# A decoder layer on one core: idle products and idle accumulating loads in the first feed-forward

## The chip, the cores and the metric

The kernel runs on one core of a Trainium2 chip. A core has engines that each work through an instruction queue of their own, in order: TensorE (PE in the profile, its weight loads PEld), VectorE (DVE), ScalarE (ACT), GpSimd (POOL) and SyncE (SP, which here only starts transfers). They wait for each other through semaphores. Transfers between the large memory and the on-chip memory are started by SP, ACT or POOL and carried out by 16 DMA engines that all queues share. The metric is the device time of one execution in microseconds (us); a lower time is better.

## The reference, cut to what matters

The layer works on 272 tokens (16 learned meta tokens and 256 of the sequence) of width 2048, in float32:

```python
s = concat([meta, x])                                   # 272 x 2048
h = rms_norm(s, norm_ffn1)
s = s + 0.5 * swiglu_ffn(h, ffn1_w_gu, ffn1_w_down)     # first feed-forward, width 5632
h = rms_norm(s, norm_mix)
q, k, v, b_gate, c_gate, u = split(h @ w_in)
y_att, y_conv = diff_attention(q, k, v, ...), short_conv(b_gate, c_gate, u, conv_w)
s = s + (sum of gated (y_att, y_conv) @ w_branch) @ w_out
h = rms_norm(s, norm_ffn2)
s = s + 0.5 * swiglu_ffn(h, ffn2_w_gu, ffn2_w_down)     # second feed-forward
return rms_norm(s, norm_final)[16:]

def swiglu_ffn(h, w_gu, w_down):
    gate, up = split(h @ w_gu)
    return (silu(gate) * up) @ w_down
```

## The kernel before

Every large product is computed from rounded halves. The type F32R is a rounded float32 that TensorE takes in one pass. Each weight block `st` is rounded on ACT to `wh` (L258) and the rest `wl = st - wh` is made on DVE (L259); activations are kept in the same way as a high and a low part. One weight chunk of 128 rows by 128 columns then needs three products: high times high (L267), high times low (L268) and low times high (L269).

`linear` does one group of 512 output columns: it goes through the 16 chunks of 128 rows of the contraction in 8 blocks of two chunks, and keeps four accumulators (one PSUM bank each) of 272 tokens. A block of two chunks is 2 x 4 x 3 = 24 products of 272 columns, and a whole `linear` is 192. The buffers `wh` and `wl` are three deep, so ACT can round block n only when TensorE is through with block n - 3. The raw block `st` is four deep, with four chunks in each.

In the first feed-forward, `gate_up` calls `linear` twice for each group g: once for the gate (accumulators `pg`) and once for the up part (`pu`). What follows a `linear` (its evict function) is put in `pending` and is emitted while the next `linear` runs, after its chunk 1 (`EVICT_AT`). Small work of another kind is put in the list `side`; each `linear` takes one entry of it after its chunks 5, 9 and 13. Below, pg0, pu0, pg1, pu1, pg2 name the first five `linear` calls in order, and pu1 block 3 the fourth block of two chunks of pu1.

In pg0 the kernel also prepares its input block by block (`before1`); with the last block it puts `make_vec` and `lam_step` in `side`. They are taken in pu0 after chunks 5 and 9. Nothing else is in `side` then until the end of the first feed-forward.

The scratch tiles of tag `wide` are three deep; `sg`, which holds the gate of one group until its up part is done, is one of them. The emitted instructions are ordered for each engine by a scheduler that works at build time. The input `s` lies in four tiles `sF`.

Of the kernel before, what the change touches and what calls it, by code (L numbers as in the profile page):

```python
# [9 lines left out]
F32 = mybir.dt.float32  # L10
F32R = mybir.dt.float32r
AF = mybir.ActivationFunctionType
ALU = mybir.AluOpType
AX = mybir.AxisListType

P = 128
# [5 lines left out]
DC = D // P  # L22
GC = 4
GW = GC * P
# [18 lines left out]
def decoder_layer(ctx: ExitStack, tc: tile.TileContext, t, out):  # L43
    nc = tc.nc

    const = ctx.enter_context(tc.tile_pool(name="const", bufs=1))
    wpool = ctx.enter_context(tc.tile_pool(name="w", bufs=W_BUFS))
    apool = ctx.enter_context(tc.tile_pool(name="a", bufs=N_ACT))
    tmp = ctx.enter_context(tc.tile_pool(name="tmp", bufs=2))
    psum = ctx.enter_context(tc.tile_pool(name="ps", bufs=8, space=bass.MemoryType.PSUM))  # L50

    def bank(name):
        return psum.tile([P, 512], F32, tag="acc", name=name)

    def wide(shape, name):
        return tmp.tile(shape, F32, tag="wide", bufs=3, name=name)
# [16 lines left out]
    def load_x(k):  # L73

        q, cs = k // 2, slice(k % 2 * GW, (k % 2 + 1) * GW)
        for i in range(2):
            nc.sync.dma_start(out=xin[q][i][:, cs], in_=x[i * P : (i + 1) * P, k * GW : (k + 1) * GW])
# [9 lines left out]
    def load_gain(g0, src):  # L87
# [5 lines left out]
        out=vrows[G_CONV:G_SUB, :], in_=t["conv_w"][0].rearrange("k (c p) -> (k c) p", p=P)  # L93
# [3 lines left out]
    for i, n in enumerate(("lambda_q1", "lambda_k1", "lambda_q2", "lambda_k2")):  # L97
# [7 lines left out]
        out=mask[:, T - P :],  # L105
        in_=mask[:, T - P :],
# [13 lines left out]
    def col(i):  # L120
        return vec[:, i : i + 1]
# [9 lines left out]
    def make_lam():  # L131
        lprod = tmp.tile([P, 2, HD], F32, tag="lprod", bufs=1, name="lprod")
        nc.vector.tensor_mul(lprod, lamv[:, 0:4:2, :], lamv[:, 1:4:2, :])
        ldot = const.tile([P, 2], F32, name="ldot")
        nc.vector.tensor_reduce(out=ldot, in_=lprod, axis=AX.X, op=ALU.add)
        lexp = const.tile([P, 2], F32, name="lexp")
        nc.scalar.activation(lexp, ldot, AF.Exp)
        nc.vector.tensor_sub(lam, lexp[:, 0:1], lexp[:, 1:2])
        nc.vector.tensor_scalar_add(lam, lam, LAM_INIT)
        nc.vector.tensor_scalar_mul(subg, col(G_SUB), 1.0 - LAM_INIT)  # L140


    sF = [apool.tile([P, GC, T], F32, tag="act", name=f"s{g}") for g in range(DC // GC)]
# [26 lines left out]
    def gain_split(h, c, gain):  # L170

        w = h.width
        hi, lo = h.part(c, 0, 0, w), h.part(c, 1, 0, w)
        a = nc.scalar.mul(hi, s(c, T - w), gain)
        b = nc.vector.scalar_tensor_tensor(
            out=lo, in0=s(c, T - w), scalar=gain, in1=hi.bitcast(F32), op0=ALU.mult, op1=ALU.subtract
        )
        return a.ins, b.ins
# [50 lines left out]
    side = []  # L229
# [179 lines left out]
    h1 = Act("h1", DC, T)  # L409
    norm1 = Norm(0, "1")  # L410

    def prep(c):
        pt = bank("pt")
        q, cs = c // NH, slice(c % NH * P, (c % NH + 1) * P)
        nc.tensor.transpose(pt[:, :NMETA], xm[q][:, cs], ident[:NMETA, :NMETA])
        for i in range(2):
            nc.tensor.transpose(pt[:, NMETA + i * P : NMETA + (i + 1) * P], xin[q][i][:, cs], ident)
        v = nc.vector.tensor_copy(s(c, 0), pt[:, :T])
        a, b = gain_split(h1, c, gain1[:, c : c + 1])
        return a, v.ins  # L420

    def before1(blk):


        c = blk[0]
        if c // 2 + 1 < 4:
            load_x(c // 2 + 1)
        r = []
        for k in blk:
            a, v = prep(k)  # L430
            r = [a, v]
        if c:
            for k in blk:
                norm1.add(k - 2)
        if c == DC - 2:
            for k in blk:
                norm1.add(k)
            pending.append(norm1.end)
            side.append(make_vec)

            def lam_step():
                with tc.issue_after(norm1.last.ins):
                    make_lam()

            side.append(lam_step)
        return r


# [3 lines left out]
    def after1(c):  # L452
        gain_split(h2, c, col(G_MIX + c))
        norm2.add(c)
        if c == DC - 1:
            side.append(norm2.end)

    for half in halves:
        m = gate_up(h1, half, t["ffn1_w_gu"][0], norm1, 0, before1 if half is halves[0] else None)
        for c in range(0, DC, GC):  # L460

            def down(pd, c=c, final=half is halves[-1]):
                for j in range(GC):
                    nc.vector.scalar_tensor_tensor(
                        out=s(c + j, 0), in0=pd[j][:, :T], scalar=0.5, in1=s(c + j, 0), op0=ALU.mult, op1=ALU.add
                    )
                    if final:
                        after1(c + j)

            linear(m, list(range(len(half) * GC)), t["ffn1_w_down"][0], half[0] * GC, c * P, 0, T, "pd", down)  # L470
# [265 lines left out]
    for half in halves:  # L736
        m = gate_up_tok(h3, half, w_gu, norm3)
        final = half is halves[-1]
        if final:
            for q in range(2):  # L740
                nc.gpsimd.dma_start(
                    out=gfin[q],
                    in_=t["norm_final"][q * W2 : (q + 1) * W2].rearrange("(o d) -> o d", o=1).to_broadcast([P, W2]),
# [46 lines left out]
```

## Time and profile before

| What | Value |
|---|---|
| time, median of 2 runs | 2233.66 us (2233.38 to 2233.95) |
| span of the profiled execution, from first to last instruction | 2231.4 us |
| what the runs' median has beside that span | 2.3 us |
| PE busy | 2215.7 us (99%), 14014 matmul records |
| DVE busy | 1268.5 us (57%) |
| ACT busy | 979.2 us (44%) |
| POOL busy | 6.4 us, 17 instructions |
| mean granted TensorE clock | 0.999 |
| moved by DMA | 401.98 MB, 180 GB/s over the span |

The profiled execution has no time of its own listed beside its span, so its own time is taken as the span and the 2.3 us around it. The trace stamps every instruction with a start and a duration. Products on TensorE are pipelined: a product is listed with some 0.29 us, though the next one begins 0.125 us later, so the cost of a product is read from start to start.

### The profile page before, as it was taken

The numbers are of one execution on the slowest core, as the hardware profiler recorded it, in microseconds if no ns is written. First come the engines' busy times: TensorE is split into PE (matmuls) and PEld (weight loads), VectorE is DVE, ScalarE is ACT, GpSimd is POOL, SyncE is SP. The second block draws the span as 40 slices with busy tenths as digits, with TensorE's granted clock in tenths as the row PEclk, the third lists the DMA queues.
The fourth block names the chain that finished last, engine by engine and source line by source line (L and its number), as shares of the span: only waits on it lengthen the run. The fifth ranks groups of instructions, "written<-read, shape, count | busy, mean of one in ns | idle before, by whom it ended". The sixth has DMA issues, their size and how long they took to land.

```text
span 2231.4 us, 33637 instructions
## 1 busy us (share of the span) xinstructions
PE 2215.7 (99%) x14014; PEld 2017.6 (90%) x14014; DVE 1268.5 (57%) x1681; ACT 979.2 (44%) x1238; POOL 6.4 (0%) x17
## 2 busy tenths in 40 slices
PE   9999999999999999999999999999999999999998
PEld 8999999999999999898988888888888888888886
DVE  7555554455555565667766665665555545455554
ACT  6444343334343443544455454544444433444443
POOL 0000000000000000000000000000000000000000
PEclk9999999999999999999999999999999999999999
DMA  7555555545555555444455555555555556555553
GB/s 232 173 181 176 171 172 181 176 170 175 181 174 170 175 178 177 151 152 151 153 195 187 188 184 192 186 189 189 188 189 189 189 189 214 199 185 192 189 182 120
DMA packets 191257, 401.98 MB, mean 180 GB/s; under 512 B 7908, under 2 KB 7968, under 8 KB 191104
## 3 DMA queue, kind: packets, MB, share of 16 engines
q1 hardware_dynamic: 190464, 398.49, 53.3%
q8 instruction: 109, 1.79, 0.3%
q0 software_dynamic: 544, 1.21, 0.2%
q14 instruction: 44, 0.36, 0.0%
q10 hardware_dynamic: 96, 0.14, 0.0%
HBM read 397.71 MB, written 2.10 MB: 179 GB/s over the span
## 4 chain that ended last, share of the span: by engine, by line
PE 99%; ACT 0%; DVE 0%; DMA 0%; issue 0%; ACTq 0%
PE pg L301 7%; PE pg L303 7%; PE pg L302 7%; PE g L265 5%; PE pg L269 4%; PE pg L267 4%; PE pd L269 4%; PE pu L269 4%; PE pu L267 4%; PE pg L268 4%; PE pd L267 4%; PE pu L268 4%; PE pd L268 4%; PE pd L303 4%; PE pd L301 4%; PE pd L302 4%
## 5 line engine op out<-in xcount | busy, mean ns | idle before, releaser
L259 DVE TENSOR_TENSOR wl<-st,wh 128x1024 fp32r<-128x1024 f32 x488 | 596.2, 1225 | 538.1 <-ACT wh L258 537.4
L258 ACT CAST wh<-st 128x1024 fp32r<-128x1024 f32 x488 | 514.0, 1054 | 731.2 <-PE pd L268 146.5
L319 DVE TENSOR_TENSOR wl<-st,wh 128x1024 fp32r<-128x1024 f32 x264 | 323.1, 1225 | 343.1 <-ACT wh L318 343.0
L318 ACT CAST wh<-st 128x1024 fp32r<-128x1024 f32 x264 | 278.6, 1055 | 411.6 <-PE pg L302 268.7
L301 PE MATMUL pg<-wh,h 128*128 128x512 f32 x704 | 276.0, 392 | 0.0
L303 PE MATMUL pg<-wl,h 128*128 128x512 f32 x704 | 274.2, 390 | 0.0
L302 PE MATMUL pg<-wh,h 128*128 128x512 f32 x704 | 273.9, 389 | 0.0
L267 PE MATMUL pg<-h,wh 128*128 128x272 f32 x704 | 203.5, 290 | 2.0 <-ACT wh L258 2.0
L267 PE MATMUL pu<-h,wh 128*128 128x272 f32 x704 | 203.2, 289 | 0.0
L269 PE MATMUL pd<-m,wl 128*128 128x272 f32 x704 | 203.0, 288 | 0.0
L269 PE MATMUL pu<-h,wl 128*128 128x272 f32 x704 | 203.0, 288 | 0.0
L267 PE MATMUL pd<-m,wh 128*128 128x272 f32 x704 | 203.0, 288 | 0.0
L268 PE MATMUL pu<-h,wh 128*128 128x272 f32 x704 | 202.4, 288 | 0.0
L268 PE MATMUL pg<-h,wh 128*128 128x272 f32 x704 | 202.4, 288 | 0.0
L268 PE MATMUL pd<-m,wh 128*128 128x272 f32 x704 | 202.4, 287 | 0.0
L269 PE MATMUL pg<-h,wl 128*128 128x272 f32 x704 | 201.2, 290 | 0.0
L265 PE MATMUL g<-h,wh 128*128 128x512 f32 x512 | 180.1, 395 | 0.0
L303 PEld LDWEIGHTS pg<-wl,h 128*128 128x128 f32 x704 | 132.1, 188 | 27.8
L302 PEld LDWEIGHTS pg<-wh,h 128*128 128x128 f32 x704 | 132.2, 188 | 26.8
L301 PEld LDWEIGHTS pg<-wh,h 128*128 128x128 f32 x704 | 132.2, 188 | 26.7
L269 PE MATMUL g<-h,wl 128*128 128x256 f32 x512 | 143.4, 280 | 0.0
L301 PE MATMUL pd<-wh,m 128*128 128x512 f32 x352 | 137.3, 390 | 0.0
(229 smaller groups left out, 4109.1 us busy)
## 6 DMA issues: line engine op xcount, KB each, us to landing
st<-in_ffn_w_gu_dram SPq DMA_DIRECT2D x184, 512.0 KB, 4.2
st<-in_ffn_w_down_dram SPq DMA_DIRECT2D x88, 1024.0 KB, 5.1
st<-in_ffn_w_gu_dram SPq DMA_DIRECT2D x84, 1024.0 KB, 4.9
st<-in_w_in_dram SPq DMA_DIRECT2D x48, 1024.0 KB, 5.1
st<-in_w_gate_dram SPq DMA_DIRECT2D x32, 1024.0 KB, 5.1
st<-in_w_branch_dram SPq DMA_DIRECT2D x16, 1024.0 KB, 5.0
st<-in_w_out_dram SPq DMA_DIRECT2D x16, 1024.0 KB, 5.0
xin<-in_x_dram SPq DMA_DIRECT2D x8, 256.0 KB, 7.3
```

The lines of the kernel that those rows point to most:

```text
L258: nc.scalar.copy(out=wh[:, :m, :], in_=sw)
L259: nc.vector.tensor_sub(wl[:, :m, :], sw, wh[:, :m, :].bitcast(F32))
L265: nc.tensor.matmul(acc[j][:, : 2 * n], wh[:, i, f], act.both(c, t0, t1), start=first, stop=False)
L267: nc.tensor.matmul(a, wh[:, i, f], act.part(c, 0, t0, t1), start=first, stop=False)
L268: nc.tensor.matmul(a, wh[:, i, f], act.part(c, 1, t0, t1), start=False, stop=False)
L269: nc.tensor.matmul(a, wl[:, i, f], act.part(c, 0, t0, t1), start=False, stop=last)
L301: nc.tensor.matmul(ps, act.part(c, 0, tok.start, tok.stop), wh[:, q, :], start=first, stop=False)
L302: nc.tensor.matmul(ps, act.part(c, 1, tok.start, tok.stop), wh[:, q, :], start=False, stop=False)
L303: nc.tensor.matmul(ps, act.part(c, 0, tok.start, tok.stop), wl[:, q, :], start=False, stop=last)
L318: nc.scalar.copy(out=wh, in_=sw)
L319: nc.vector.tensor_sub(wl, sw, wh.bitcast(F32))
```

## The change

When the last block of pg0 is prepared, six more entries are put in `side`, behind `make_vec` and `lam_step`. None of them computes anything that the output uses; each writes one column of a small tile `sink`. Four entries issue products of the activations h1 with themselves into a fresh PSUM bank: 24 of 136 columns, 24 of 128 columns, 16 pairs of 272 and 136 columns, and 16 of 64 columns. Every product has another stationary operand than the one ahead of it, and each entry ends with a copy of one column by DVE. The other two entries each have three steps of this kind: ACT fills a `wide` tile with -1 times a column of s, POOL starts a transfer of 512 KB of weights that is added to what is in the tile, and DVE copies one column of it. In the second entry the tile has type F32R.

By the places in `side`, the entries are taken at pu0 chunk 13, at pg1 chunks 5, 9 and 13, and at pu1 chunks 5 and 9.

```diff
             side.append(lam_step)
+            book()
         return r
...
+    sink = const.tile([P, 4], F32, name="sink")
+
+    def idle(k, form, count):
+        def f():
+            ps = bank("idle")
+            for i in range(count):
+                c, d = (3 * i) % DC, (3 * i + 1) % DC
+                lhs = h1.part(d, i % 2, 0, P)
+                if form == "short":
+                    nc.tensor.matmul(ps[:, :136], lhs, h1.part(c, 0, 136, 272), start=True, stop=True)
+                elif form == "short128":
+                    nc.tensor.matmul(ps[:, :128], lhs, h1.part(c, 0, 128, 256), start=True, stop=True)
+                elif form == "short64":
+                    nc.tensor.matmul(ps[:, :64], lhs, h1.part(c, 0, 128, 192), start=True, stop=True)
+                elif form == "mixed":
+                    nc.tensor.matmul(ps[:, :272], lhs, h1.both(c, 0, 136), start=True, stop=False)
+                    nc.tensor.matmul(ps[:, :136], h1.part(c, 0, 0, P), h1.part(c, 0, 0, 136), start=False, stop=True)
+            nc.vector.tensor_copy(sink[:, k : k + 1], ps[:, 0:1])
+
+        return f
+
+    def loads(cast):
+        def f():
+            for i in range(3):
+                at = wide([P, 2, GW], "at")
+                if cast:
+                    at = tmp.tile([P, 2, GW], F32R, tag="wide", bufs=3, name="atr")
+                src = t["ffn2_w_gu"][0][i * P : (i + 1) * P, 0 : 2 * GW].rearrange("p (q f) -> p q f", q=2)
+                nc.scalar.mul(at, h1.tiles[i][:, 0, :, 0:1].bitcast(F32).to_broadcast([P, 2, GW]) if 0 else sF[i][:, 0:2, 0:1].to_broadcast([P, 2, GW]), -1.0)
+                nc.gpsimd.dma_start(out=at, in_=src, accum_op=ALU.add)
+                nc.vector.tensor_copy(sink[:, 3:4], at[:, 0, 0:1].bitcast(F32) if cast else at[:, 0, 0:1])
+
+        return f
+
+    def book():
+        side.extend([idle(0, "short", 24), idle(1, "short128", 24), idle(2, "mixed", 16), idle(0, "short64", 16), loads(False), loads(True)])
```

TensorE's queue, in pu0 between chunk 13 and chunk 14. The name behind the arrow is what is read; `wh` and `wl` are the weight halves, `h_...` the activations. Of the 24 rows of L468 the first three and the last are shown:

```order
L269 MATMUL pu_576<-h_128,wl 128x272
L468 MATMUL idle<-h_122 128x136
L468 MATMUL idle<-h_123,h_124 128x136
L468 MATMUL idle<-h_125 128x136
L468 MATMUL idle<-h_124,h_125 128x136
L267 MATMUL pu_573<-h_129,wh 128x272 [waits Activation_49]
```

Before, the row of L267 stood right behind that of L269. The other three entries stand in the same way behind chunks 5, 9 and 13 of pg1.

ACT's queue before, from the rounding of pu1 block 2 to that of block 4 (L359 is the sigmoid of the gate of pg1):

```order
L258 CAST wh<-st 128x1024 [waits DMAHW4_49,PE_49,Activation_49]
L359 ACTIVATE sgm<-gt 128x272 [waits DVE_49]
L359 ACTIVATE sgm<-gt 128x272 [waits DVE_49,Activation_49]
L258 CAST wh<-st 128x1024 [waits PE_49]
L359 ACTIVATE sgm<-gt 128x272 [waits DVE_49,Activation_49]
L258 CAST wh<-st 128x1024 [waits DMAHW5_49,PE_49]
```

The same stretch of ACT's queue with the change, from the rounding of block 2 on. DMASW0 to DMASW5 are the semaphores of the six accumulating loads, DMAHW those of the weight loads. The five roundings L258 in it are those of pu1 blocks 2 to 6:

```order
L258 CAST wh<-st 128x1024 [waits DMAHW4_49,PE_49,Activation_49]
L487 ACTIVATE at<-s_118 128x1024
L359 ACTIVATE sgm<-gt 128x272 [waits DVE_49,Activation_49] x2
L487 ACTIVATE at<-s_119 128x1024
L258 CAST wh<-st 128x1024 [waits PE_49]
L258 CAST wh<-st 128x1024 [waits DMAHW5_49,PE_49]
L487 ACTIVATE at<-s_120 128x1024 [waits DMASW0_49,DVE_49]
L487 ACTIVATE atr<-s_118 128x1024 [waits DMASW1_49,DVE_49]
L258 CAST wh<-st 128x1024 [waits PE_49,Activation_49]
L487 ACTIVATE atr<-s_119 128x1024 [waits DMASW2_49,DVE_49]
L258 CAST wh<-st 128x1024 [waits DMAHW6_49,PE_49,Activation_49]
L487 ACTIVATE atr<-s_120 128x1024 [waits DMASW3_49,DVE_49]
```

The first two fills find a free buffer; from the third on each waits for an accumulating load and for DVE's copy of it, and the roundings of blocks 5 and 6 stand behind such waits.

DVE's queue with the change, from the low half of pu1 block 3 to that of pg2 block 0; before, it held these six rows of L259 and, behind the first, two rows of the gate (L360, L361) and nothing else:

```order
L259 TENSOR_TENSOR wl<-st,wh 128x1024 [waits PE_49,Activation_49]
L489 COPY sink<-at 128x1 [waits DMASW0_49]
L259 TENSOR_TENSOR wl<-st,wh 128x1024 [waits DMAHW5_49,PE_49,Activation_49]
L489 COPY sink<-at 128x1 [waits DMASW1_49,DVE_49]
L259 TENSOR_TENSOR wl<-st,wh 128x1024 [waits PE_49,Activation_49]
L489 COPY sink<-at 128x1 [waits DMASW2_49,DVE_49]
L489 COPY sink<-atr 128x1 [waits DMASW3_49,DVE_49]
L259 TENSOR_TENSOR wl<-st,wh 128x1024 [waits DMAHW6_49,PE_49,Activation_49]
L259 TENSOR_TENSOR wl<-st,wh 128x1024 [waits PE_49,Activation_49]
L489 COPY sink<-atr 128x1 [waits DMASW4_49,DVE_49]
L489 COPY sink<-atr 128x1 [waits DMASW5_49,DVE_49]
L259 TENSOR_TENSOR wl<-st,wh 128x1024 [waits DMAHW7_49,PE_49,Activation_49]
```

The low halves of pu1 block 4 and later now stand behind copies that wait for accumulating loads. Outside pu0, pg1, pu1 and the start of pg2 the queues of all engines hold the same instructions in the same order as before.

## The prediction

> **What bounds the kernel now.** I read the head of the page first: span, busy time by engine, granted clock, and the chain that ended last.
>
> ```profile
> span 2231.4 us, 33637 instructions
> PE 2215.7 (99%) x14014; PEld 2017.6 (90%) x14014; DVE 1268.5 (57%) x1681; ACT 979.2 (44%) x1238; POOL 6.4 (0%) x17
> PEclk9999999999999999999999999999999999999999
> PE 99%; ACT 0%; DVE 0%; DMA 0%; issue 0%; ACTq 0%
> ```
>
> The chain is TensorE's queue, from end to end, at full clock. So whatever is put into that queue, and every microsecond in which it waits, comes out at the end one for one; what DVE, ACT, POOL or the DMA engines are given costs nothing until TensorE waits for it. Busy shares say little more, so I go to the timeline of the stretch that is changed. A `linear` of 192 products of 272 columns runs from the first `pu` product of pu1 to the first `pg` product of pg2:
>
> ```profile
> 92.25 0.29 PE L267 MATMUL pu<-h,wh 128*128 128x272 f32 x1
> ...
> 116.35 0.29 PE L267 MATMUL pg<-h,wh 128*128 128x272 f32 x1
> ```
>
> That is 24.10 us for 192, 0.1255 us for each and 3.01 us for a block of 24, without a gap.
>
> **The change, first part: 96 idle products, all on the path.** The order shows them inside TensorE's queue with products of the chain behind them. Sixteen have 272 columns and cost 0.1255 each. Eighty have 136, 128 or 64 columns of the one-pass type, and the trace has no such product. The nearest rows are the transposes of 128 columns, which also take a new stationary operand of 128x128 each time, put between products of 512 columns:
>
> ```profile
> 1547.99 0.39 PE L301 MATMUL pg<-wh,h 128*128 128x512 f32 x1
> 1548.45 0.39 PE L303 MATMUL pg<-wl,h 128*128 128x512 f32 x1
> 1548.68 0.60 PE L401 MATMUL mt_ps<-ident,mt 128*128 128x128 f32 x4
> 1549.03 0.47 PE L301 MATMUL pg<-wh,h 128*128 128x512 f32 x1
> 1549.34 0.39 PE L302 MATMUL pg<-wh,h 128*128 128x512 f32 x1
> ```
>
> Two products of 512 columns take 0.46 (1547.99 to 1548.45). From L303 at 1548.45 to L302 at 1549.34 are 0.89, in which two such products and four transposes go: 0.43 for four, **0.108** each. The three other values to weigh:
>
> - Columns alone. 272 columns take 0.1255 and 512 take 0.23, 0.44 ns a column and some 0.007 besides; so 136, 128 and 64 columns would take 0.067, 0.063 and 0.035. Sum: 24 x 0.067 + 24 x 0.063 + 16 x (0.1255 + 0.067) + 16 x 0.035 = **6.8 us**.
> - The floor of the transposes, 0.108 for every narrow product: 24 x 0.108 + 24 x 0.108 + 16 x (0.1255 + 0.108) + 16 x 0.108 = **10.7 us**.
> - Four times the column time, as a plain float32 product has. The sum of squares L198 is one:
>
> ```profile
> 43.05 0.29 PE L269 MATMUL pg<-h,wl 128*128 128x272 f32 x1
> 43.18 0.62 PE L198 MATMUL ssq_ps<-ssq,ones 128*128 128x272 f32 x2
> 43.76 0.29 PE L268 MATMUL pu<-h,wh 128*128 128x272 f32 x1
> ```
>
> From 43.05 to 43.76 are 0.71; two products of 0.1255 are in it, so 0.46 for 272 columns, 1.69 ns a column: 0.230, 0.216 and 0.108 for 136, 128 and 64 columns. Sum: 5.5 + 5.2 + 16 x 0.3555 + 1.7 = **18.1 us**.
>
> I take 10.7: the transposes are the rows nearest in width and in having a new stationary operand each time, and they show a rate that no narrower column count explains. 6.8 and 18.1 stay as ends. The four copies to `sink` (DVE waits for the products) stand behind a low half that DVE finishes about 2.8 us after a block's end (1.05 of rounding, 1.23 of subtracting, handovers), about when the idle products end; DVE's next row can't start before the next block ends, so they are covered. The fourth accumulator of pg1 now waits for DVE, but the three ahead of it give it nine products, 1.1 us, of cover.
>
> **Second part: six accumulating loads.** They add no product. They put fills into ACT's queue and waiting copies into DVE's, and behind these stand the weight halves that TensorE takes one block per 3.01 us. These rows of ACT and DVE give the starting point and the durations:
>
> ```profile
> L259 DVE TENSOR_TENSOR wl<-st,wh 128x1024 fp32r<-128x1024 f32 x488 | 596.2, 1225 | 538.1 <-ACT wh L258 537.4
> L258 ACT CAST wh<-st 128x1024 fp32r<-128x1024 f32 x488 | 514.0, 1054 | 731.2 <-PE pd L268 146.5
> 92.00 0.43 ACT L359 ACTIVATE sgm<-gt 128x272 f32<-128x272 f32 x1 [1.65 <-DVE gt L357]
> 92.36 1.06 ACT L258 CAST wh<-st 128x1024 fp32r<-128x1024 f32 x1
> 95.33 1.06 ACT L258 CAST wh<-st 128x1024 fp32r<-128x1024 f32 x1 [0.86 <-PE pu L268]
> 101.36 1.06 ACT L258 CAST wh<-st 128x1024 fp32r<-128x1024 f32 x1 [1.96 <-PE pu L268]
> 50.16 0.15 DVE L139 TENSOR_SCALAR lam<-lam 128x1 f32<-128x1 f32 x1
> ```
>
> Rounding takes 1.05, the low half 1.23, a one-column DVE step 0.15; a fill of 1024 columns isn't in the trace and I give it the 1.05 of the rounding, of the same engine and shape. ACT is idle for 1.96 before a rounding, so a fill costs nothing by its length. In before's clock (the shift of the first part moves all alike): two sigmoids from 92.0, the rounding of block 2, then the first fill, which ends at 94.9; sigmoids and the second fill end at 96.8.
>
> Call L the time from POOL's issue to the landing. With 0.1 for the handover to POOL and 0.2 for DVE's copy and the way back (estimates from the 0.15 row), the third fill may start at 94.9 + 0.1 + L + 0.2 = 95.2 + L. It takes 1.05; its load lands at 96.35 + 2L, so the fifth fill starts at 96.55 + 2L. Then follow, on ACT, that fill, the rounding of pu1 block 6 (done at 98.65 + 2L) and the sixth fill (done at 99.7 + 2L). The sixth load lands at 99.8 + 3L, DVE copies (0.15), and only then makes the low half of pg2 block 0: **101.2 + 3L**. TensorE needs it two products into pg2, at 116.60. So the stall is **3L - 15.4** us, nothing below L = 5.1. Part of it shows earlier: TensorE wants pu1 block 6 at 110.3. Behind the low half of pg2 block 0, DVE has room again (1.23 of each 3.01 us) and gives nothing further back or away.
>
> What is L? No accumulating load is in the trace. These are the nearest:
>
> ```profile
> DMA to landing us min/median/max: 5.3/5.5/5.7
> DMA to landing us min/median/max: 3.3/4.9/8.2
> 1867.70 0.56 POOL L741 DMA_DIRECT2D gfin<-in_norm_final_dram  x1 [1861.44 <-PE pd L303]
> st<-in_ffn_w_gu_dram SPq DMA_DIRECT2D x184, 512.0 KB, 4.2
> st<-in_ffn_w_gu_dram SPq DMA_DIRECT2D x84, 1024.0 KB, 4.9
> out_dram<-sT SPq DMA_DIRECT2D x4, 512.0 KB, 3.3
> ```
>
> The first row is that of `gfin`: POOL's own 512 KB loads, beside weight loads, took **5.5**, of which POOL spent 0.56 on issuing. The second row is that of all weight loads. The accumulating load also reads its destination, another 512 KB; on SP's queue the second 512 KB cost 0.7 (4.2 to 4.9). Two accumulating loads overlap here, so I count that twice: 5.5 + 1.4, **L = 7.0** rounded (estimate). Ends: 3.3, the fastest 512 KB of any queue (no stall), and 11.0, twice `gfin`, if reading and adding run at half its pace (stall 17.6). At 7.0 the stall is 3 x 7.0 - 15.4 = **5.6 us**: a gap of 98.65 + 14.0 - 110.3 = 2.3 before pu1 block 6, about 1 for its low half, and the rest ahead of pg2 block 0. The 3.1 MB more for the DMA engines I cost at nothing: weight loads land in 4.9 and their buffers reach 8 blocks ahead, 24 us; if that cover went, each late block would cost TensorE its lateness.
>
> **Sum.** 10.7 + 5.6 = 16.3 us. The durations come from an execution with a span of 2231.4; the runs' median of 2233.66 has 2.3 us around that, which the change leaves alone. So 2233.66 + 16.3 = **2250.0 us**.
>
> **The rivals.**
>
> - The loads are hidden. With L below 5.1 the copies never hold up TensorE: 2233.7 + 10.7 = 2244.4. For it: SP's 512 KB loads land in 4.2. Against it: POOL's own took 5.5 without adding. The Trainium skill, "DMA: Bandwidth & Descriptors", section "Anatomy of one DMA — SWDGE (gpsimd) path", gives a DMA from this queue about 2.0 us and its bytes over 436 GB/s, an estimate of 3.2 us for 512 KB, which would be this case; the trace's 5.5 disagrees. 12%.
> - Narrow products pay four times the column time: 18.1 in place of 10.7, 2257.4. For it: the kernel's float32 products do, at 1.69 ns a column. Against it: these are of the one-pass type, at 0.44 ns. 14%.
> - The clock falls in the gap. The only long wait of TensorE is at the start, and its first products came at half pace:
>
> ```profile
> 9.48 0.59 PE L267 MATMUL pg<-h,wh 128*128 128x272 f32 x1 [2.02 <-ACT wh L258]
> 13.18 0.34 PE L267 MATMUL pg<-h,wh 128*128 128x272 f32 x1
> ```
>
>   From 9.48 to 13.18 are 15 products in 3.70 us, 1.8 more than at 0.1255. If a gap before pu1 block 6 (over 3 us from L = 7.4 on) does that again, it adds 1.8, or 3.6 with a second one: with L = 8, 10.7 + 8.6 + 1.8 gives 2254.8. For it: that start; against it: products had hardly run before it. 10%. The Trainium skill, "TensorE: Matmul & The Clock Gate", section "Why this matters for your kernels", sets the limit at idle gaps of about 3 us, after which the clock is halved; no row here shows such a gap in mid-run.
> - Slower by over 2%: the accumulation itself is slow, three times `gfin` or more. The place is the same chain of three loads; 2% is 44.7 us, 34.0 of it stall, so it decides from L = 16.5. At L = 22 the stall is 50.6 and the time 2295. For it: nothing here shows the pace of adding in a transfer, and half the loads also change type on the way. Against it: all weight loads stay within 8.2. 9%.
> - The idle products don't do what they say, slipping into pauses that TensorE has: 2234 to 2240. Against it: 24.10 us for 192 products leaves no pause. 3%.
>
> **How the numbers follow.** The forecast keeps 52%. The range is 2241 (columns alone, no stall: 2240.5) to 2272 (18.1 with L = 11 is 2269.4, and a fall of the clock on top). Outside lie the slow loads (9%), the idle products without effect (3%) and the ends of the others (some 6%). Two per cent is about what a measurement of this kernel can tell from no change: over 2278.3 is 9%, under 2189.0 1%, 90% between.
>
> **What would show it.** The idle rows from start to start: 0.108 confirms the floor, 0.07 or 0.22 the ends. POOL's loads from issue to landing: L. TensorE waiting for `wh` before pu1 block 6 and for `wl` in pg2 block 0, by 2 to 3 us each, and DVE waiting for the loads in L489; no wait at all confirms the first rival, and one in another `linear` would mean that I have missed a queue. I am wrong if L is far from 7, or if narrow products don't all cost alike.

## The result, and the profile after

| | before | changed |
|---|---|---|
| time, median | 2233.66 us (2233.38 to 2233.95, 2 runs) | 2250.45 us (2250.42 to 2250.48, 2 runs) |
| ratio to before | | 1.0075 (95% interval 1.0046 to 1.0104) |
| span of the profiled execution | 2231.4 us | 2248.7 us |
| mean granted TensorE clock | 0.999 | 0.997 |

The forecast was 2250.0 us within 2241 to 2272; the kernel is 16.8 us slower. The changed kernel was timed again later, beside other kernels on one chip: 2251.64 us there, before 2232.96, ratio 1.0085 (1.0071 to 1.0099).

Busy times by engine and the chain that ended last, from the changed kernel's page:

```profile
PE 2228.6 (99%) x14110; PEld 2030.2 (90%) x14110; DVE 1270.0 (56%) x1691; ACT 982.1 (44%) x1244; POOL 11.5 (1%) x23
PE 93%; DMA 0%; DVE 0%; ACT 0%; issue 0%; DVEq 0%
```

TensorE has 96 records more (14014 to 14110), as many as there are idle products, and 12.9 us more of busy time. DVE and ACT have only 1.5 and 2.9 us more. The chain is still TensorE's queue: the view follows it back from the end to a load that POOL started at 123.60 and no further, so the first 5.5% of the span are in no share.

The idle products, by the timeline of TensorE. First those of 136 columns in pu0, then the first pair of 272 and 136 in pg1, then the end of those of 64 columns:

```profile
64.39 0.29 PE L269 MATMUL pu<-h,wl 128*128 128x272 f32 x1
64.58 0.28 PE L468 MATMUL idle<-h,h 128*128 128x136 f32 x1
67.03 0.27 PE L468 MATMUL idle<-h,h 128*128 128x136 f32 x1
67.32 0.29 PE L268 MATMUL pu<-h,wh 128*128 128x272 f32 x1
...
88.13 0.34 PE L474 MATMUL idle<-h,h 128*128 128x272 f32 x1
88.31 0.22 PE L475 MATMUL idle<-h 128*128 128x136 f32 x1
88.37 0.34 PE L474 MATMUL idle<-h 128*128 128x272 f32 x1
...
98.98 0.28 PE L472 MATMUL idle<-h 128*128 128x64 f32 x1
99.32 0.28 PE L472 MATMUL idle<-h,h 128*128 128x64 f32 x1
```

The second and the last of the 24 products of 136 columns are shown: from 64.58 to 67.03 are 2.45 us for 22 steps: 0.111 each. Those of 64 columns take the same (98.98 to 99.32 are three steps of 0.113). In a pair the next product begins only 0.06 behind the start of the 136 columns, but 0.18 behind that of the 272 columns ahead of them: 0.24 for both. From L269 at 64.39 to L268 at 67.32 are 2.93 us; two products of 0.1255 belong there anyway, so the entry adds 2.68. Read in the same way, the other three add 2.69, 3.76 and 1.78: **10.9 us** together.

TensorE's waits, and the two places where they lie:

```profile
PE warm L64 <- POOL ident masks.py:199: 2.4, 1, 2.4
PE pg L269 <- DVE wl L259: 2.4, 1, 2.4
PE pu L269 <- DVE wl L259: 2.2, 1, 2.2
PE pg L267 <- ACT wh L258: 2.0, 1, 2.0
```
```profile
120.48 0.29 PE L269 MATMUL pu<-h,wl 128*128 128x272 f32 x1
121.01 0.29 PE L268 MATMUL pu<-h,wh 128*128 128x272 f32 x1
123.48 0.39 PE L269 MATMUL pu<-h,wl 128*128 128x272 f32 x1 [2.18 <-DVE wl L259]
123.83 0.29 PE L268 MATMUL pu<-h,wh 128*128 128x272 f32 x1
...
129.47 0.29 PE L268 MATMUL pg<-h,wh 128*128 128x272 f32 x1
132.12 0.55 PE L269 MATMUL pg<-h,wl 128*128 128x272 f32 x1 [2.36 <-DVE wl L259]
132.47 0.43 PE L267 MATMUL pg<-h,wh 128*128 128x272 f32 x1
135.41 0.38 PE L268 MATMUL pg<-h,wh 128*128 128x272 f32 x1
135.64 0.29 PE L269 MATMUL pg<-h,wl 128*128 128x272 f32 x1
```

The first and the fourth line of the waits are those of the start, in before too. The two others are new: for the low half of pu1 block 6 and of pg2 block 0. From 120.48 to 123.83 are 3.35 us where five products take 0.63: **2.7 us**. From 129.47 to 135.64 are 6.17 where 16 steps take 2.01: 4.16, of which the wait is 2.65 - 0.13 = **2.5** and products at half pace (0.226 from start to start, 132.47 to 135.41) are the other **1.6**. The granted clock, which the profile lists by stretch, is 0.50 from 132.2 to 135.4 and 1.00 from 123.5 to 127.0, behind the first wait; so the half pace is the clock.

Who is late is seen in the rows of the loads and copies (timeline of POOL, ACT and DVE; `at` and `atr` landed after 5.6 to 6.8 and 6.9 to 7.5 us):

```profile
106.67 0.87 POOL L488 DMA_DIRECT2D at<-in_ffn_w_gu_dram  x1 [0.67 <-ACT at L487]
115.10 0.85 POOL L488 DMA_DIRECT2D atr<-in_ffn_w_gu_dram  x1 [2.00 <-ACT atr L487]
119.70 1.03 ACT L258 CAST wh<-st 128x1024 fp32r<-128x1024 f32 x1
122.06 0.15 DVE L489 COPY sink<-atr 128x1 f32<-128x1 f32 x1 [3.36 <-DMA atr<-in_ffn_w_gu_dram]
123.60 0.85 POOL L488 DMA_DIRECT2D atr<-in_ffn_w_gu_dram  x1 [2.67 <-DVE wl L259]
130.71 0.15 DVE L489 COPY sink<-atr 128x1 f32<-128x1 f32 x1 [2.85 <-DMA atr<-in_ffn_w_gu_dram]
130.84 2.36 DVE L259 TENSOR_TENSOR wl<-st,wh 128x1024 fp32r<-128x1024 f32 x2
```

These are the second, fourth and sixth load, issued at 106.67, 115.10 and 123.60, the last two each behind a fill that waited for the copy of the one before: 8.5 us a round. The rounding of pu1 block 6 (119.70) makes TensorE only 0.2 late, but DVE makes its low half only behind the copy of 122.06. The last copy comes at 130.71, and DVE makes the low half of pg2 block 0 only then.

**The ledger**: 10.9 + 2.7 + 4.2 = 17.8 us, against 17.3 of span. The rest is the start. TensorE began pu0 at 43.43 in the trace of before and at 42.83 here, since its first product of pg0 began 0.6 us sooner (8.88 against 9.48), ahead of anything that the change adds; pu0 began anywhere from 42.46 to 44.22 in the ten traces of this study. So below, beside the time, stands the span counted **from the start of pu0** and compared with before's 2231.4 - 43.43 = 2187.97. For the changed kernel that is 2248.7 - 42.83 - 2187.97 = 17.9, which the ledger fills.

### The profile page after: what moved, and what is told of

Same layout as the page of the kernel before. It is cut to its first block, busy times and chain, and to the rows that moved or that the text cites. A ratio compares the mean times of both kernels' runs of the same rounds, so it can differ in the third digit from the quotient of the medians.

```text
span 2248.7 us, 33870 instructions
## 1 busy us (share of the span) xinstructions
PE 2228.6 (99%) x14110; PEld 2030.2 (90%) x14110; DVE 1270.0 (56%) x1691; ACT 982.1 (44%) x1244; POOL 11.5 (1%) x23
## 4 chain that ended last, share of the span: by engine, by line
PE 93%; DMA 0%; DVE 0%; ACT 0%; issue 0%; DVEq 0%
PE pg L301 7%; PE pg L303 7%; PE pg L302 7%; PE g L265 5%; PE pd L269 4%; PE pd L267 4%; PE pd L268 4%; PE pd L302 3%; PE pd L301 3%; PE pd L303 3%; PE pg L269 3%; PE pg L267 3%; PE pu L269 3%; PE pg L268 3%; PE pu L267 3%; PE pu L268 3%
## 5 line engine op out<-in xcount | busy, mean ns | idle before, releaser
L259 DVE TENSOR_TENSOR wl<-st,wh 128x1024 fp32r<-128x1024 f32 x488 | 595.9, 1224 | 535.4 <-ACT wh L258 534.8
L258 ACT CAST wh<-st 128x1024 fp32r<-128x1024 f32 x488 | 512.0, 1050 | 728.6 <-PE pd L268 146.9
L267 PE MATMUL pg<-h,wh 128*128 128x272 f32 x704 | 204.3, 291 | 2.0 <-ACT wh L258 2.0
L269 PE MATMUL pu<-h,wl 128*128 128x272 f32 x704 | 203.4, 289 | 2.2 <-DVE wl L259 2.2
L269 PE MATMUL pg<-h,wl 128*128 128x272 f32 x704 | 202.2, 292 | 2.5 <-DVE wl L259 2.4
L267 PE MATMUL pu<-h,wh 128*128 128x272 f32 x704 | 203.7, 289 | 0.0
L269 PE MATMUL pd<-m,wl 128*128 128x272 f32 x704 | 203.3, 289 | 0.0
L268 PE MATMUL pg<-h,wh 128*128 128x272 f32 x704 | 203.2, 290 | 0.0
L267 PE MATMUL pd<-m,wh 128*128 128x272 f32 x704 | 203.2, 289 | 0.0
L268 PE MATMUL pu<-h,wh 128*128 128x272 f32 x704 | 202.7, 288 | 0.0
L268 PE MATMUL pd<-m,wh 128*128 128x272 f32 x704 | 202.7, 288 | 0.0
L303 PEld LDWEIGHTS pg<-wl,h 128*128 128x128 f32 x704 | 132.2, 188 | 27.8
L269 PE MATMUL g<-h,wl 128*128 128x256 f32 x512 | 143.7, 281 | 0.0
```

The costliest lines, as they stand in the source:

```text
L258: nc.scalar.copy(out=wh[:, :m, :], in_=sw)
L259: nc.vector.tensor_sub(wl[:, :m, :], sw, wh[:, :m, :].bitcast(F32))
L267: nc.tensor.matmul(a, wh[:, i, f], act.part(c, 0, t0, t1), start=first, stop=False)
L268: nc.tensor.matmul(a, wh[:, i, f], act.part(c, 1, t0, t1), start=False, stop=False)
L269: nc.tensor.matmul(a, wl[:, i, f], act.part(c, 0, t0, t1), start=False, stop=last)
L303: nc.tensor.matmul(ps, act.part(c, 0, tok.start, tok.stop), wl[:, q, :], start=False, stop=last)
```

## The experiments

All are built from the changed kernel; "from pu0" is the difference just explained, from one trace each. Before took 2233.30 us beside the four kernels from "products alone" on, and 2232.96 beside the last four of the table.

| Kernel | Time, median us | Ratio to before (95%) | from pu0, us |
|---|---|---|---|
| changed, first trace | 2250.45 | 1.0075 (1.0046 to 1.0104) | +17.9 |
| products alone | 2244.49 | 1.0049 (1.0034 to 1.0064) | +11.1 |
| loads alone | 2240.03 | 1.0031 (1.0020 to 1.0042) | +5.6 |
| loads alone, without adding | 2233.21 | 1.0000 (0.9991 to 1.0010) | +0.2 |
| changed, 20 more products ahead of pg2, in a bank apart | 2250.64 | 1.0076 (1.0059 to 1.0093) | +17.1 |
| changed, 20 more products into the bank of pg2 | 2250.01 | 1.0077 (1.0064 to 1.0089) | +16.3 |
| changed, again | 2251.64 | 1.0085 (1.0071 to 1.0099) | +20.5 |
| loads alone, eight in place of six | 2243.61 | 1.0046 (1.0030 to 1.0061) | +10.9 |
| narrow products alone, 64 stationary columns | 2237.50 | 1.0019 (1.0010 to 1.0028) | +4.2 |

The theory: the products are a pure insertion at a floor per product, and the loads make DVE late by a chain of three rounds. The first pair of runs takes the change apart.

**Products alone.**

```diff
-        side.extend([idle(0, "short", 24), idle(1, "short128", 24), idle(2, "mixed", 16), idle(0, "short64", 16), loads(False), loads(True)])
+        side.extend([idle(0, "short", 24), idle(1, "short128", 24), idle(2, "mixed", 16), idle(0, "short64", 16)])
```

> Only the four entries of idle products, no loads. Theory: the two parts add up, and the products are a pure insertion of 0.111 us each (0.236 for a pair of 272 and 136): 10.9 us over before, 2244.6, no wait of TensorE beyond the two at the start. Rival: part of the 16.8 us is something else that the products bring (other PSUM banks, DVE copies that hold up low halves); then this kernel is more than 12 us over before, or the loads alone account for more than 6.5 us.

Measured: 2244.49 us, 11.1 from pu0, and by the view of waits TensorE waits nowhere but for the 2.4 and 2.0 us of the start, as before. The insertion is pure; banks and DVE's copies cost nothing that shows.

**Loads alone.**

```diff
-        side.extend([idle(0, "short", 24), idle(1, "short128", 24), idle(2, "mixed", 16), idle(0, "short64", 16), loads(False), loads(True)])
+        side.extend([lambda: None] * 4 + [loads(False), loads(True)])
```

> Only the six accumulating loads, at the same places of pu1; the four other entries do nothing. Theory: the chain of three rounds (fill, transfer of about 7.0 us, copy) makes DVE late, with two waits of TensorE of 2 to 2.5 us, before the low half of pu1 block 6 and of pg2 block 0: 5.3 us, and up to 1.6 more for a clock that falls behind a wait; 5 to 7 us over before, 2239 to 2241. Rival: the loads are late only because the products change the order ahead of them; then under 3 us.

Measured: 2240.03 us in the median, 5.6 from pu0. The waits, beside the two of the start:

```profile
PE pu L267 <- ACT wh L258: 1.6, 1, 1.6
PE pg L269 <- DVE wl L259: 1.5, 1, 1.5
PE pu L269 <- DVE wl L259: 1.5, 1, 1.5
```

Three waits where two were expected, and each shorter: ACT's rounding of pu1 block 6 is itself late here. No slow products follow in this trace (granted clock 1.00 from 111 to 116); from start to start the three places cost 1.8 us each, so the 5.6 are waits alone. The trace is that of the fastest of seven executions (2237.84 to 2242.10 us), and the median is 6.7 over before. Products and loads alone are 11.1 + 5.6 = 16.7 from pu0, or 11.2 + 6.7 = 17.9 by the medians, against 17.9 and 20.5 from pu0 and 16.8 and 18.7 by the medians for the changed kernel. So the parts add up within what executions differ by; that the slow products are what the changed kernel has on top holds for the traces compared here only.

**The loads without adding.**

```diff
-                nc.gpsimd.dma_start(out=at, in_=src, accum_op=ALU.add)
+                nc.gpsimd.dma_start(out=at, in_=src)
```

> As the kernel with the loads alone, but the six transfers overwrite the tile and don't add to it. Theory that reading the destination and adding make up the length: the landing falls to about the 5.5 us of gfin, three rounds are 4.5 us shorter, and the stall shrinks to about 1 us (0 to 2): 2234 to 2236. Rival, that the length comes from POOL's queue and from the weight loads beside it: landing stays near 7.0 us and the kernel is as slow as that with the accumulating loads.

Measured: ratio 1.0000, 0.2 from pu0, no wait of TensorE behind the start. The rows of `atr` of this kernel and of that with the loads alone (first issuing, then landing):

```profile
L488 POOL DMA_DIRECT2D atr<-in_ffn_w_gu_dram x3: 527/527/530, 103.5 to 109.8; - x3
DMA to landing us min/median/max: 4.6/5.3/5.7
```
```profile
L488 POOL DMA_DIRECT2D atr<-in_ffn_w_gu_dram x3: 847/854/854, 104.4 to 113.3; - x3
DMA to landing us min/median/max: 6.2/6.5/7.2
```

Adding costs 1.2 us of landing in the median of `atr` and 2.6 in that of `at` (4.9 against 7.5), of which 0.3 is POOL's longer issuing. The landing falls to that of `gfin` or below, and the same chain with it fits into the slack: the mechanism, and that adding is what makes L long enough to matter, are shown. What the change of type to F32R costs is not told apart: `atr` landed sooner than `at` in the median with the loads alone (6.5 against 7.5), but later in the changed kernel's first trace (7.0 against 6.2) and without adding (5.3 against 4.9), and the two entries run at different times.

**More products into the wait.** If TensorE waits at pg2 and then runs slowly, products that fill the wait are free. The first version:

```diff
+            if h is h1 and g == 2:
+                fill = bank("fill")
+                for i in range(20):
+                    nc.tensor.matmul(fill[:, :128], h.part((3 * i + 1) % DC, i % 2, 0, P), h.part((3 * i) % DC, 0, 128, 256), start=True, stop=True)
             linear(h, list(range(DC)), w_gu, 0, g * GW, 0, n, "pg", gate, before=before)
```

> The changed kernel with 20 more idle products of 128 columns (2.2 us by 0.111 each) in TensorE's queue right ahead of pg2, where it waited 2.4 us for the low half of pg2 block 0 and its next 14 products came at half pace (1.6 us). Theory: the products fit in the wait, so they cost nothing, the low half comes when it came before, and the clock stays up: 1.0 to 1.6 us faster than the changed kernel (2248.9 to 2249.5). Rival, that the slow pace is not a matter of TensorE's idleness: same time as the changed kernel or up to 2.2 us slower.

Measured: 2250.64 us, no difference from the changed kernel that can be told, and 17.1 from pu0. The clock stayed up behind the wait, but the bank that `fill` takes is missing for the fourth accumulator of pg2, which now waits for DVE to empty one of pu1 (beside a wait of 1.9 for the low half of pu1 block 6):

```profile
PE pg L267 <- DVE sg L365: 0.3, 1, 0.3
PE pg L269 <- DVE wl L259: 0.2, 1, 0.2
```

So this version was inconclusive. The second writes into the first accumulator of pg2, which its first real product overwrites:

```diff
         acc = [bank(f"{name}_{j}") for j in range(GC)]
+        for i in range(fill):
+            nc.tensor.matmul(acc[0][:, :128], act.part((3 * i + 1) % DC, i % 2, 0, P), act.part((3 * i) % DC, 0, 128, 256), start=True, stop=True)
```

> As the kernel with 20 more idle products ahead of pg2, but these write into the first accumulator of pg2, which its first real product then overwrites, so that no bank is waited for (that wait cost 0.5 us). Theory: the products lie within the wait and keep the clock up; counted from the start of pu0, 1.0 to 1.8 us faster than the changed kernel although TensorE has 2.2 us more to do. Rival: the wait does not absorb them, up to 2.2 us slower.

It ran beside the changed kernel again:

> The changed kernel once more, on the same chip as the runs beside it. The products of pu0 began at 42.83 us in its first trace and at 43.43 in that of before, and the start has differed by up to 1.7 us between the traces so far. Theory: 10.9 of products, 5 to 5.5 of waits and up to 1.6 of slow clock, so 16.5 to 18 us over before counted from the start of pu0; slow products behind a wait of over 2.4 us. Rival: the slow products behind the second wait were chance; then 16 us and none of them.

Measured: 2250.01 us with the 20 products and 2251.64 without, on the same chip; 16.3 and 20.5 from pu0. The intervals of the two ratios overlap (1.0064 to 1.0089, 1.0071 to 1.0099), so that the time is shorter is likely but not shown; that 2.2 us more of work cost nothing is (2249.09 to 2251.22 in five executions with the products, 2251.01 to 2253.85 in four without). From pu0 the 16.3 are 1.6 below the first trace's 17.9, as expected; the 20.5 are of the slowest of the four. The timelines at the start of pg2, with the products and then without:

```profile
129.69 0.22 PE L241 MATMUL pg<-h 128*128 128x128 f32 x1
131.75 0.28 PE L241 MATMUL pg<-h,h 128*128 128x128 f32 x1
132.04 0.29 PE L270 MATMUL pg<-h,wh 128*128 128x272 f32 x1
132.23 0.39 PE L271 MATMUL pg<-h,wl 128*128 128x272 f32 x1
```
```profile
134.42 0.59 PE L269 MATMUL pg<-h,wl 128*128 128x272 f32 x1 [4.16 <-DVE wl L259]
139.12 0.43 PE L268 MATMUL pg<-h,wh 128*128 128x272 f32 x1
139.34 0.43 PE L269 MATMUL pg<-h,wl 128*128 128x272 f32 x1
```

With the products no real product of pg2 waits or runs slowly, and the granted clock is 1.00 from 130 to 136: keeping TensorE busy kept the clock up here. Without them this trace had a longer wait than the first one, since two of the `atr` loads landed after 8.8 us (6.4 to 8.8), and it was followed by products at 0.227 for over 5 us. So the 20.5 are 2.6 us above the first trace's 17.9, outside the 16.5 to 18 expected: L differs from one execution to the next, and three rounds and the clock multiply that. The slow products stand behind this wait in both traces of the changed kernel, so they were hardly chance.

**Eight loads in place of six.**

```diff
-            for i in range(3):
+            for i in range(4):
                 at = wide([P, 2, GW], "at")
```

> The loads alone, with four steps in each entry in place of three: eight loads, four rounds. Theory: a round is a transfer of about 7 us and 1.5 us of fill, copy and handover, so the low half of pg2 block 1 comes after a fourth transfer; less the 3.0 us a block that TensorE works between, 4 to 5 us more than with three (5.6 from the start of pu0): 9.5 to 11, and with waits of over 2.5 us the clock falls and adds 1.6 each: 9.5 to 13 us over before. Rival: the waits are a matter of the DMA engines' load and not of the rounds; then the stall grows by a third, to 7.5 us.

Measured: 10.9 from pu0, 5.3 over the six loads and within the 9.5 to 13 expected; by the medians the step is 2243.61 - 2240.03 = 3.6. Its longer waits for ACT and DVE:

```profile
PE pg L267 <- ACT wh L258: 5.1, 2, 3.1
PE pu L269 <- DVE wl L259: 1.2, 1, 1.2
PE pu L267 <- ACT wh L258: 0.8, 1, 0.8
```

(2.0 of the first line are the start.) Here products ran at half pace behind the waits of 0.8 and 1.2, which lie within 2.8 us of each other, and again behind that of 3.1. Read from start to start, some 6 of the 10.9 us are waits and 4.7 slow products, where six loads had 5.4 and none. So the waits grew by less than 1 us, less than a fourth round (4 to 5) and less than a third more (1.9), and while its products run slowly TensorE comes later to the next block, and so waits less for it. The time alone therefore doesn't decide between the rounds and the load of the DMA engines. The rows of the copies of the fourth and the sixth load, and of the sixth and the eighth load themselves, speak for the rounds:

```profile
111.96 0.15 DVE L489 COPY sink<-at 128x1 f32<-128x1 f32 x1 [2.36 <-DMA at<-in_ffn_w_gu_dram]
113.50 0.86 POOL L488 DMA_DIRECT2D atr<-in_ffn_w_gu_dram  x1 [1.67 <-ACT atr L487]
121.79 0.15 DVE L489 COPY sink<-atr 128x1 f32<-128x1 f32 x1 [2.75 <-DMA atr<-in_ffn_w_gu_dram]
123.33 0.86 POOL L488 DMA_DIRECT2D atr<-in_ffn_w_gu_dram  x1 [2.06 <-ACT atr L487]
```

Each load from the third on is issued 1.5 us behind the copy of the load two before it.

**Half as many stationary columns.** What is the floor of 0.111 us?

```diff
-                lhs = h1.part(d, i % 2, 0, P)
+                lhs = h1.part(d, i % 2, 0, 64)
...
-                    nc.tensor.matmul(ps[:, :136], lhs, h1.part(c, 0, 136, 272), start=True, stop=True)
+                    nc.tensor.matmul(ps[:64, :136], lhs, h1.part(c, 0, 136, 272), start=True, stop=True)
```

The products of 128 and 64 columns are changed in the same way, the pairs and the loads left out.

> The narrow idle products alone (24 of 136, 24 of 128, 16 of 64 columns; no pairs and no loads) with a stationary operand of 64 columns in place of 128. Theory: the 0.111 us that all three widths took is the load of 128 stationary columns; with 64 it falls to about 0.055, and the products pay the larger of that and their own columns: 24 x 0.067 + 24 x 0.063 + 16 x 0.055 = 4.0 us from the start of pu0. Rival: 0.111 is a floor of each product, whatever is loaded: 64 x 0.111 = 7.1 us.

Measured: 4.2 from pu0, against 4.0 and 7.1. The first and the last of each kind, and what follows on those of 128:

```profile
65.91 0.23 PE L468 MATMUL idle<-h 128*64 128x136 f32 x1
67.36 0.23 PE L468 MATMUL idle<-h,h 128*64 128x136 f32 x1
...
79.54 0.22 PE L470 MATMUL idle<-h 128*64 128x128 f32 x1
80.98 0.34 PE L267 MATMUL pg<-h,wh 128*128 128x272 f32 x1
...
93.09 0.19 PE L472 MATMUL idle<-h 128*64 128x64 f32 x1
93.93 0.22 PE L472 MATMUL idle<-h,h 128*64 128x64 f32 x1
```

1.45 us for 23 steps of 136 columns are 0.063 each, 1.44 for 24 of 128 are 0.060, 0.84 for 15 of 64 are 0.056. With 128 stationary columns all were 0.111. So the floor goes with the stationary operand, some 0.056 for 64 columns and 0.111 for 128, and the products' own columns decide only above it. That it is the loading of the operand fits best; the result has half as many rows here too, and no run has narrow products that keep their stationary operand, which would part the two.

## Why the prediction was right

- **What bounds the kernel.** Right: what was put into TensorE's queue and what it waited for came out at the end one for one (17.8 of ledger, 17.9 from pu0).
- **The products: 10.7, measured 10.9.** The transposes were the right row. They share with the idle products that each has 128 new stationary columns, and the floor goes with these (half of it with 64). Columns alone (6.8) and four times the column time (18.1) were both wrong for 128 stationary columns; the rival with four times fell. Copies and banks cost nothing, as said.
- **The chain of loads: 5.6, measured 2.7 + 2.5 = 5.2.** L was 7.0 by estimate; the medians were 6.2 for `at` and 7.0 for `atr`, and the two rounds shown took 7.0 and 7.1 from issue to copy. The terms behind the estimate fit less well than their sum: without adding the medians were 4.9 and 5.3 in place of 5.5, and adding cost 1.2 to 2.6 in place of 1.4. The mechanism came as forecast, and TensorE stood at the two blocks that were named, but one wait was put on the wrong engine: before pu1 block 6 it was to wait 2.3 for ACT's `wh` and 1 for the low half, and the cost was 0.2 and 2.5. Two details of the chain were off, and cancelled: a fill reached POOL's issue after 0.3, not 0.1, and the chain that ended last went through the second, fourth and sixth load, since their landings were the longer ones, not through the first, third and sixth with the rounding of block 6 between.
- **The clock: a rival with 10%, not in the sum, but it occurred.** It added 1.6 in the first trace and 2.7 in the second. It came at pg2, not at pu1 block 6, after a wait shorter than I had set (2.65 us from start to start, by the rows above) and was absent behind one nearly as long (2.47). Behind the waits of 0.8 and 1.2 close together with eight loads it came too, yet behind the 1.6 and 1.5 at the same place with six, which lie 2.0 us apart, it did not. Neither the length of a wait nor two waits close together tell; what sets it off stays open. The Trainium skill, "TensorE: Matmul & The Clock Gate", section "Why this matters for your kernels", with its limit of about 3 us was thus no safe bound here; its section "Part 1: The HAM clock gate" calls the window free-running, which would fit, but no run here shows the window itself.
- **Why the time still fits so closely.** In part this is luck. In the first trace the start happened to be 0.6 us shorter; that and the 0.4 less of waits offset a good part of the 1.6 of slow clock and the 0.2 of products. Another 0.5 lies in the 2.3 us around the span: the executions of before that have both listed took 1.8 over their span, as the changed kernel did, so the traced one was some 0.5 below the median of 2233.66. With the second timing (2251.64, 18.7 over before) the sum is 2.4 short, about the size of the term left out (2.7 in that kernel's trace).
- **The loads hidden.** That is what the chain does with L at 4.9 to 5.3, as the loads without adding show. The Trainium skill's rule for this queue, "DMA: Bandwidth & Descriptors", section "Anatomy of one DMA — SWDGE (gpsimd) path", 3.2 us by estimate for 512 KB, is below what plain loads took (3.8 to 5.7) and less than 60% of what adding ones did (5.5 to 8.8).
- **Slow loads** (L of 16.5 or more) and **products without effect** fell.

## What to carry to other kernels

Where one engine is the chain, an idle product with a new stationary operand costs the larger of its own columns and a floor that goes with the stationary columns (0.111 us for 128 here), however narrow it is. A transfer in the middle of an in-order queue is paid not once but as often as its buffer is reused before the consumer runs dry: count the rounds, then the slack, and look for the copy that stands ahead of work that others need. After a forced wait look at the pace of the next products too, since the clock can take its share: here 1.6 us behind a wait of 2.5, and 2.7 behind one of 4.3.

## What the runs showed of the hardware that was not expected

- Adding in a transfer of 512 KB cost 1.2 to 2.6 us in the medians of landing (5.3 to 6.5 for `atr`, 4.9 to 7.5 for `at`), and POOL's issuing rose from 0.53 to 0.85 us. In one execution two of the six adding loads took 8.8 us.
- TensorE's half pace came behind waits of 0.8 and 1.2 us within 2.8 us of each other, and did not come behind single ones of 2.2 (first trace) and 2.3 us (that with 20 products into the bank of pg2), nor behind 1.6 and 1.5 us that lie 2.0 us apart (loads alone). The stretches at a granted clock of 0.50 lasted from 3.3 us (first trace) to 6.4 us (eight loads, behind the wait of 3.1).
- The start of the kernel differs by up to 1.8 us between traces (pu0 from 42.46 to 44.22), which is more than several of the effects here; spans had to be counted from pu0.
